# Two chained matrix products on one core: the first product's operands from bfloat16 to float32r

## Chip, cores, metric

One NeuronCore of a Trainium2 chip. The metric is device time in microseconds (us), from profiled and unprofiled executions of the whole kernel; lower is better. Unless said otherwise, the *pitch* of matmuls is the distance between the start times of neighbouring matmul records in the trace, and a *full-clock* pitch is one taken where the records of the granted TensorE clock stand at 1.0.

## The reference

```python
# x (16, 512, 768), w1 (768, 3072), b1 (3072), w2 (3072, 768), all float32
y = np.matmul(x, w1) + b1
y = np.maximum(y, 0)
return np.matmul(y, w2).astype(np.float32)
```

## The kernel before

The 8192 rows of x go through in 16 blocks of 512. Per block: 24 transposes of 128x128 on the TensorE (PE) bring x into the layout that the PE contracts over, the VectorE (DVE) copies them from PSUM to SBUF, 144 matmuls make the first product (24 tiles of hidden units, 6 steps of contraction), the ScalarE (ACT) adds the bias and applies the ReLU, and 192 matmuls make the second product. Everything that the PE reads is bf16; the loads on the gpsimd queue cast.

```python
w1_sb = const_pool.tile([P, KS, H], BF16)
ident = const_pool.tile([P, P], BF16)
xload_pool: bufs=8   xt_pool: bufs=3   yt_pool: bufs=2   osb_pool: bufs=6
tr_psum:    bufs=2   mm1_psum: bufs=2  mm2_psum: bufs=4      # PSUM

def load_xblock(blk):                       # 4 tiles of 128 rows
    xl = xload_pool.tile([P, K], BF16, name="xl")
    nc.gpsimd.dma_start(out=xl, in_=xf[m0 + ms * P: ..., :])

def transpose_xblock(xls):
    xt = xt_pool.tile([P, KS, M_BLK], BF16, name="xt")
    for ms in range(MSUB):                  # 4 groups
        trp = tr_psum.tile([P, KS, P], BF16, name="trp")
        for k in range(KS):                 # 6 transposes each
            nc.tensor.transpose(trp[:, k, :],
                                xls[ms][:, k * P:(k + 1) * P], ident)
        nc.vector.tensor_copy(out=xt[:, :, ms * P:(ms + 1) * P], in_=trp)
    return xt

def mm1(xt):
    for ht in range(HS):                    # 24
        for k in range(KS):                 # 6
            nc.tensor.matmul(ps, lhsT=w1_sb[:, k, ht * P:(ht + 1) * P],
                             rhs=xt[:, k, :], start=(k == 0), stop=(k == KS - 1))
        nc.scalar.activation(out=yt[:, ht, :], in_=ps, func=Relu, bias=...)
# mm2: 4 output tiles of 48 matmuls of 384 columns, two DVE copies, one DMA each
# ... cut ...
for blk in range(NBLK):
    xt = transpose_xblock(xls_next.pop(0))
    if blk + 2 < NBLK:
        xls_next.append(load_xblock(blk + 2))
    yt = mm1(xt)
    mm2(blk, yt)
```

(The pool lines are shortened here.)

## Time and profile before

1066.14 us (median of 2 runs, 1066.07 to 1066.21). The numbers that matter:

| in the steady state, per block of 65.0 us | us |
|---|---|
| boundary: first transpose to first matmul of the first product | 2.72 |
| first product, 144 matmuls at a pitch of 216 ns | 31.08 |
| second product, 192 matmuls at a pitch of 162.5 ns | 31.20 |

Sixteen such blocks are 1040 us; the other 26 us are the start (first x; then matmuls at half clock, 427 ns apart up to 14.7 us; waiting for w2) and the end. The clock's records begin only at 14.7 us, so the row PEclk below does not show that first stretch.

The page of the profile, its busy times, its chain of waits (the work that ended last, followed back) and the costliest groups. A group line has line, engine, operation, output<-inputs, shapes and count, then busy us, mean ns of one, and the idle time of the engine before them with what ended it.

```profile
PE 1033.2 (97%) x5760; PEld 551.0 (52%) x5760; DVE 96.9 (9%) x192; ACT 265.2 (25%) x385; POOL 67.1 (6%) x118
...
PEclk9999999999999999999999999999999999999999
...
PE 91%; DMA 4%; DVE 3%; POOL 1%; issue 0%; DVEq 0%; POOLq 0%
PE mm2p L112 46%; PE mm1p L95 44%; DMA w_sb<-in_w_dram 4%; DVE osb L117 1%; DVE xt L77 1%; POOL w_sb L82 1%; PE trp L75 1%; POOL xl L65 0%; DVEq L162 0%; POOL ident masks.py:199 0%; POOL ident masks.py:197 0%; POOLq masks.py:199 0%; POOLq L151 0%
...
L112 PE MATMUL mm2p<-w_sb,yt 128*128 128x384 bf16 x3072 | 506.2, 327 | 6.8 <-DMA w_sb<-in_w_dram 6.3
L95 PE MATMUL mm1p<-xt,w_sb 128*128 128x512 bf16 x2304 | 502.1, 380 | 3.9 <-DVE xt L77 3.9
...
L117 DVE COPY osb<-mm2p 128x384 f32<-128x384 f32 x128 | 65.3, 551 | 945.0 <-PE mm2p L112 945.0
...
L75 PE MATMUL trp<-ident,xl 128*128 128x128 bf16 x384 | 30.2, 224 | 17.6 <-DVE xt L77 11.2
L75 PEld LDWEIGHTS <-xl 128*128 128x128 bf16 x384 | 24.8, 100 | 23.6 <-issue 13.0
L77 DVE COPY xt<-trp 128x768 bf16<-128x768 bf16 x64 | 32.8, 549 | 20.4 <-PE trp L75 18.6
```

The PE is busy 97% of the span and 90% of the chain that ended last are the two products. The mean of a matmul record (380 ns) is longer than its pitch, since matmuls overlap in the pipeline; that is why pitches are used here. A stretch of the first product in the timeline (start, duration, group, count) shows it: 20 matmuls in 4.48 us, so (4.48 - 0.38) / 19 = 216 ns each. The Trainium skill, "TensorE: Matmul & The Clock Gate", section "Back-to-back issue gap", gives N / 2.4 + 2.5 ns for the gap of an isolated matmul of N moving columns at full clock, 215.8 for 512, and about 131 ns for 512 columns in a stream of weight loads and matmuls: this trace is such a stream, and agrees with the first figure, not with the second.

```profile
299.76 4.48 PE L95 MATMUL mm1p<-xt,w_sb 128*128 128x512 bf16 x20
```

One boundary, from the timeline of before:

```profile
214.83 1.63 PE L112 MATMUL mm2p<-w_sb,yt 128*128 128x384 bf16 x9
...
216.30 0.83 PE L75 MATMUL trp<-ident,xl 128*128 128x128 bf16 x12
216.34 1.02 DVE L117 COPY osb<-mm2p 128x384 f32<-128x384 f32 x2 [6.78 <-PE mm2p L112]
...
217.27 2.15 DVE L77 COPY xt<-trp 128x768 bf16<-128x768 bf16 x4
...
217.87 0.96 PE L75 MATMUL trp<-ident,xl 128*128 128x128 bf16 x12 [0.74 <-DVE xt L77]
...
219.02 2.32 PE L95 MATMUL mm1p<-xt,w_sb 128*128 128x512 bf16 x10 [0.18 <-DVE xt L77]
```

Two groups of transposes go at once, because there are two PSUM buffers; the DVE first copies the last output tiles, then four transposed tiles without a gap. The PE waits 0.74 and 0.18 us. One of the four groups belongs already to the next block, which is why the first product can start before the fourth copy ends.

### The profile page before, as it was taken

How to read it: one execution, taken by the hardware profiler on the slowest of the kernel's cores; microseconds unless marked ns; L12 is line 12 of the kernel's file. 1: busy time of each engine (PE TensorE's matmuls, PEld its weight loads, DVE VectorE, ACT ScalarE, POOL GpSimd, SP SyncE). 2: the span in 40 equal slices, each digit the busy share in tenths (PEclk: the TensorE clock that was granted, in tenths of full speed). 3: DMA queues.
4: the chain of work that ended last, by engine and by line, in shares of the span. 5: the costliest groups of instructions: out<-in, count | busy, mean ns of one | idle time of the engine just before them, and what ended most of it. 6: DMA issues, size and time to landing. Idle time of an engine off the chain costs nothing.

```text
span 1066.0 us, 12515 instructions
## 1 busy us (share of the span) xinstructions
PE 1033.2 (97%) x5760; PEld 551.0 (52%) x5760; DVE 96.9 (9%) x192; ACT 265.2 (25%) x385; POOL 67.1 (6%) x118
## 2 busy tenths in 40 slices
PE   7889999999999999999999999999999999999998
PEld 3344554645546455454555545455464554545554
DVE  1011010110101101020010101101011010100101
ACT  3303205032140412305123050321404214041230
POOL 7510000000000000000000000000000000000000
PEclk9999999999999999999999999999999999999999
DMA  9962030120301202011020201203012020100001
GB/s 158 195 129 60 16 75 1 45 45 15 75 1 45 45 30 60 1 54 37 30 60 15 69 7 43 47 16 74 1 46 45 19 64 1 45 15 31 30 1 60
DMA packets 43844, 48.00 MB, mean 45 GB/s; under 512 B 24336, under 2 KB 35600, under 8 KB 43792
## 3 DMA queue, kind: packets, MB, share of 16 engines
q0 software_dynamic: 31488, 22.03, 14.2%
q1 hardware_dynamic: 12304, 25.18, 6.3%
q8 instruction: 45, 0.74, 0.3%
q14 instruction: 7, 0.06, 0.0%
HBM read 44.05 MB, written 25.17 MB: 65 GB/s over the span
## 4 chain that ended last, share of the span: by engine, by line
PE 91%; DMA 4%; DVE 3%; POOL 1%; issue 0%; DVEq 0%; POOLq 0%
PE mm2p L112 46%; PE mm1p L95 44%; DMA w_sb<-in_w_dram 4%; DVE osb L117 1%; DVE xt L77 1%; POOL w_sb L82 1%; PE trp L75 1%; POOL xl L65 0%; DVEq L162 0%; POOL ident masks.py:199 0%; POOL ident masks.py:197 0%; POOLq masks.py:199 0%; POOLq L151 0%
## 5 line engine op out<-in xcount | busy, mean ns | idle before, releaser
L112 PE MATMUL mm2p<-w_sb,yt 128*128 128x384 bf16 x3072 | 506.2, 327 | 6.8 <-DMA w_sb<-in_w_dram 6.3
L95 PE MATMUL mm1p<-xt,w_sb 128*128 128x512 bf16 x2304 | 502.1, 380 | 3.9 <-DVE xt L77 3.9
L99 ACT ACTIVATE yt<-mm1p,b_sb 128x512 bf16<-128x512 f32 x384 | 263.9, 687 | 759.6 <-PE mm1p L95 759.6
L112 PEld LDWEIGHTS <-yt 128*128 128x128 bf16 x3072 | 301.1, 98 | 211.0 <-issue 12.3
L95 PEld LDWEIGHTS <-w_sb 128*128 128x128 bf16 x2304 | 225.7, 98 | 275.4 <-issue 8.1
L117 DVE COPY osb<-mm2p 128x384 f32<-128x384 f32 x128 | 65.3, 551 | 945.0 <-PE mm2p L112 945.0
L65 POOL DMA_DIRECT2D xl<-in_x_dram x64 | 34.1, 538 | 785.5 <-PE trp L75 780.4
L75 PE MATMUL trp<-ident,xl 128*128 128x128 bf16 x384 | 30.2, 224 | 17.6 <-DVE xt L77 11.2
L75 PEld LDWEIGHTS <-xl 128*128 128x128 bf16 x384 | 24.8, 100 | 23.6 <-issue 13.0
L77 DVE COPY xt<-trp 128x768 bf16<-128x768 bf16 x64 | 32.8, 549 | 20.4 <-PE trp L75 18.6
L82 POOL DMA_DIRECT2D w_sb<-in_w_dram x24 | 19.7, 836 | 5.2 <-DMA w_sb<-in_w_dram 4.6
L87 POOL DMA_DIRECT2D w_sb<-in_w_dram x24 | 12.7, 531 | 10.7 <-DMA w_sb<-in_w_dram 10.7
L99 ACT ACT_TABLE_LOAD x1 | 1.3, 1283 | 6.1 <-DMA b_sb<-in_b_dram 6.1
masks.py:199 POOL TENSOR_SCALAR_AFFINE_SELECT ident<-ident 128x128 bf16<-128x128 bf16 x1 | 0.3, 306 | 0.1
masks.py:197 POOL MEMSET ident<- 128x128 bf16 x1 | 0.2, 205 | 0.3 <-POOLq L151 0.3
L151 POOL MEMSET const-float32-0.0<- 128x1 f32 x1 | 0.1, 99 | 0.2 <-issue 0.2
L151 POOL MEMSET const-bfloat16-1.0<- 128x1 bf16 x1 | 0.1, 103 | 0.0
L151 POOL MEMSET const-uint8-127<- 128x1 uint8 x1 | 0.1, 103 | 0.0
L151 POOL MEMSET const-float32-1.0<- 128x1 f32 x1 | 0.1, 99 | 0.0
## 6 DMA issues: line engine op xcount, KB each, us to landing
out_dram<-osb SPq DMA_DIRECT2D x64, 384.0 KB, 2.3
xl<-in_x_dram POOLq DMA_DIRECT2D x64, 192.0 KB, 5.3
w_sb<-in_w_dram POOLq DMA_DIRECT2D x48, 192.0 KB, 7.8
b_sb<-in_b_dram SPq DMA_DIRECT2D x1, 12.0 KB, 5.3
```

The source lines that it names most:

```text
L65: nc.gpsimd.dma_start(out=xl, in_=xf[m0 + ms * P: m0 + (ms + 1) * P, :])
L75: nc.tensor.transpose(trp[:, k, :], xls[ms][:, k * P:(k + 1) * P], ident)
L77: nc.vector.tensor_copy(out=xt[:, :, ms * P:(ms + 1) * P], in_=trp)
L82: nc.gpsimd.dma_start(out=w1_sb[:, :, ht * P:(ht + 1) * P], in_=w1r[:, :, ht * P:(ht + 1) * P])
L87: nc.gpsimd.dma_start(out=w2_sb[:, h, :], in_=w2[h * P:(h + 1) * P, :])
L95: nc.tensor.matmul(ps, lhsT=w1_sb[:, k, ht * P:(ht + 1) * P], rhs=xt[:, k, :], start=(k == 0), stop=(k == KS - 1))
L99: nc.scalar.activation(out=yt[:, ht, :], in_=ps, func=mybir.ActivationFunctionType.Relu, bias=b1_sb[:, ht:ht + 1])
L112: nc.tensor.matmul(pss[j], lhsT=yt[:, h, ms * P:(ms + 1) * P], rhs=w2_sb[:, h, j * NF:(j + 1) * NF], start=(h == 0), stop=(h == HS - 1))
L117: nc.vector.tensor_copy(out=osb[:, j * NF:(j + 1) * NF], in_=pss[j])
L151: nc = _bacc.Bacc("TRN2", target_bir_lowering=False, num_devices=1)
```

## The change

Its intent: the first product is to read its operands at more than bf16's precision, as float32r. x is then loaded and transposed as float32, and w1 is kept as float32r. The wider tiles need room, so pools shrink: a transposed group of 6 x 128 columns takes 3072 bytes of PSUM per partition instead of 1536, and there is one such buffer instead of two.

```diff
-    w1_sb = const_pool.tile([P, KS, H], BF16)
+    w1_sb = const_pool.tile([P, KS, H], FP32R)
-    ident = const_pool.tile([P, P], BF16)
+    ident = const_pool.tile([P, P], FP32)
-    xload_pool ... bufs=8      xt_pool ... bufs=3      osb_pool ... bufs=6
+    xload_pool ... bufs=4      xt_pool ... bufs=2      osb_pool ... bufs=4
-    tr_psum ... bufs=2
+    tr_psum ... bufs=1
-            xl = xload_pool.tile([P, K], BF16, name="xl")
-            nc.gpsimd.dma_start(
+            xl = xload_pool.tile([P, K], FP32, name="xl")
+            nc.sync.dma_start(
-        xt = xt_pool.tile([P, KS, M_BLK], BF16, name="xt")
+        xt = xt_pool.tile([P, KS, M_BLK], FP32R, name="xt")
-            trp = tr_psum.tile([P, KS, P], BF16, name="trp")
+            trp = tr_psum.tile([P, KS, P], FP32, name="trp")
```

(Pool lines shortened.)

## The prediction

> **What bounds it now.** The TensorE. The page gives PE 97% busy; the chain of waits is 46% second product (L112), 44% first product (L95). In the steady state a block takes 65.0 us (start times in the trace): a boundary of 2.72 us (24 transposes, waiting for DVE copies), 144 matmuls of the first product at a start-to-start pitch of 216 ns = 31.1 us, 192 of the second at 162.5 ns = 31.2 us. 16 x 65.0 = 1040; the other 26 us are the start: first x tile at 5.9 us, cold matmuls, and about 11 us of the first block's second product waiting for w2. Weight loads (PEld, 98 ns each) are hidden.
>
> **What the change does.** It removes nothing from the PE.
>
> 1. First product, 2304 matmuls (all critical). I expect the pitch to stay near 216 ns (single pass). The risk is the weight load: the Trainium skill, "TensorE: Matmul & The Clock Gate", section on weight-path perf modes, says Fast Weight Load is on when the number of weights is 128 and the dtype is not FP32, and no run here shows where float32r falls. An unaccelerated load still hides behind 216 ns if it can be pulled ahead; if not, I estimate 55 to 110 ns more per matmul, 15 blocks x 144 = +119 to +238 us. Hiding 65%, exposure 27%, a half-rate moving stream (about +450 us) 8%.
>
> 2. Transposes are now true float32 (x and identity); now 56 ns pitch warm. Its "FP8 and Floating Point Precision", TensorE Precision Notes, gives true FP32 four passes; if that holds for transposes, about 224 ns each (estimate: 4 x 56), six per tile 1.3 us.
>
> 3. The PSUM copy goes from bf16 768 (546 ns) to f32 768. The f32 384 copy takes 551 ns, so with some 150 ns fixed I estimate 950 ns.
>
> 4. One transpose buffer instead of two: transposes and copies strictly alternate, and the instruction order shows that the group transposed ahead for the next block is gone. The boundary becomes about 4 x (1.3 + 0.95 + 0.05) = 9.2 us instead of 2.7 (7 if transposes take one pass, 13 if their weight loads are exposed too). +6.5 us x 15 = +97 us (range +62 to +160).
>
> 5. Clock: a boundary of 7 to 9 us with a thinly used array may lower the granted clock for a 3.4 us window, as once in before at 62.5 us, while w2 was awaited: 0 to 2 us per block, +10 us in sum.
>
> 6. x loads by the SP queue: off the path. The first block's end is set by w2's arrival (about 62 us, same HBM bytes), so block 0 hides up to about 11 us of slower work; hence 15 blocks, not 16.
>
> **Sum:** 1066 + 97 + 10 + a little for weight loads = about 1185 us; 8 in 10 within 1130 to 1360. Faster by over 2%: 1%; within 2%: 2%; slower: 97%.
>
> **What would show it.** Pitch of L96 matmuls (216 or about 300); count and pitch of transposes (384 or more records); DVE copy near 950 ns; wait of the transposes for DVE near 16 x 4 us, from 11 us in all; first transpose of a block to its first matmul 9 us; PEclk below 9 at block starts.
>
> **What would make it wrong.** Weight loads of float32r not overlapped (1300 to 1420 us); a half-rate moving operand (1600); transposes in a fast single pass (1140).

## The result

1222.38 us (median of 2 runs, 1221.99 to 1222.78) against 1066.14: the ratio is 1.1465, with a 95% interval of 1.1443 to 1.1487. Here and below a ratio is the mean time of one kernel's fast runs over that of the other's of the same rounds, so it is not quite the ratio of the medians quoted.

The page after, the same lines as above, and the weight loads of the first product:

```profile
PE 1139.3 (93%) x5760; PEld 801.3 (66%) x5760; DVE 125.3 (10%) x192; ACT 265.1 (22%) x385; POOL 33.2 (3%) x54
...
PEclk9979999989899898998989999899998989989899
...
PE 88%; DVE 6%; DMA 5%; issue 1%; POOL 0%; DVEq 0%; POOLq 0%
PE mm1p L96 44%; PE mm2p L113 40%; DMA w_sb<-in_w_dram 5%; DVE xt L78 5%; PE trp L76 4%; DVE osb L118 1%; POOL w_sb L83 0%; POOL w_sb L88 0%; DVEq L163 0%; POOL ident masks.py:199 0%; POOL ident masks.py:197 0%; POOLq masks.py:199 0%; POOLq L163 0%; POOLq L152 0%
...
L96 PE MATMUL mm1p<-xt,w_sb 128*128 128x512 f32 x2304 | 568.5, 409 | 16.8 <-DVE xt L78 16.8
L96 PEld LDWEIGHTS mm1p<-xt,w_sb 128*128 128x128 f32 x2304 | 451.0, 197 | 132.5 <-DVE xt L78 22.6
L113 PE MATMUL mm2p<-w_sb,yt 128*128 128x384 bf16 x3072 | 511.2, 328 | 4.3 <-DMA w_sb<-in_w_dram 3.7
...
L118 DVE COPY osb<-mm2p 128x384 f32<-128x384 f32 x128 | 65.4, 552 | 1024.6 <-PE mm2p L113 1024.6
L76 PE MATMUL trp<-ident,xl 128*128 128x128 f32 x384 | 65.1, 314 | 55.5 <-DVE xt L78 51.0
L76 PEld LDWEIGHTS trp<-ident,xl 128*128 128x128 f32 x384 | 49.6, 159 | 68.7 <-DVE xt L78 62.8
L78 DVE CAST xt<-trp 128x768 fp32r<-128x768 f32 x64 | 61.1, 955 | 67.0 <-PE trp L76 67.0
```

Read against before: PE busy time fell from 97% to 93% of a longer span, the transposes now have 55.5 us of idle time before them (17.6 before), and DVE copies went from 549 to 955 ns. The row PEclk (the granted clock, in tenths; it was 9 in every slice before) has a 7 in block 0 and from there on 8s among its 9s (a block takes two and a half slices). The second product kept its count and its mean (328 ns).

The same stretch of the first product in the timeline: 19 matmuls in 4.59 us, (4.59 - 0.39) / 18 = 233 ns each.

```profile
119.63 4.59 PE L96 MATMUL mm1p<-xt,w_sb 128*128 128x512 f32 x19
```

One boundary after. Transposes and copies take strict turns: each group of six waits about a microsecond for the copy of the one before, since there is one buffer.

```profile
165.74 2.76 PE L113 MATMUL mm2p<-w_sb,yt 128*128 128x384 bf16 x16
...
168.34 0.82 PE L76 MATMUL trp<-ident,xl 128*128 128x128 f32 x6
...
169.31 0.95 DVE L78 CAST xt<-trp 128x768 fp32r<-128x768 f32 x1
...
170.32 0.87 PE L76 MATMUL trp<-ident,xl 128*128 128x128 f32 x6 [1.16 <-DVE xt L78]
...
171.23 0.96 DVE L78 CAST xt<-trp 128x768 fp32r<-128x768 f32 x1 [0.97 <-PE trp L76]
...
172.24 0.87 PE L76 MATMUL trp<-ident,xl 128*128 128x128 f32 x6 [1.05 <-DVE xt L78]
...
176.09 5.08 PE L96 MATMUL mm1p<-xt,w_sb 128*128 128x512 f32 x14 [1.05 <-DVE xt L78]
```

From 168.34 to 176.09 is 7.75 us, where before took 2.72. Then the clock. One block of the changed kernel in three stretches (boundary, first product, second product); the columns are the stretch, its length, busy us and count of PE, PEld, DVE, ACT and POOL, and then the granted clock, the DMA share and GB/s:

```profile
317.81:326.23 8.42, 4.11 (x25) 3.00 (x24) 4.76 (x6) 0.00 (x0) 0.00 (x0) 0.84 0.67 189
326.23:361.84 35.61, 35.61 (x144) 28.43 (x145) 0.00 (x0) 15.81 (x23) 0.00 (x0) 0.94 0.04 11
361.84:393.05 31.21, 31.21 (x193) 18.85 (x193) 3.07 (x6) 0.69 (x1) 0.00 (x0) 1.00 0.10 39
```

A mean of 0.84 over 8.42 us and 0.94 over 35.61 us means a clock at one half during about 2.7 and 4.3 us: the records show one stretch of 6.83 us at 0.5, across the start of the first product. Such stretches follow 13 of the 15 boundaries after the first block, 3.41, 6.83 or 10.24 us long. In the records of before, none follows a boundary. (In block 0, while w2 is awaited, the clock is lowered for 17.1 us in the changed kernel and 3.4 us in before.)

Added up from the start times, over the whole profiled span (1065.9 to 1220.9, +155.0 us):

| where | before | after | difference |
|---|---|---|---|
| block 0 with the start, up to the first transpose of block 1 | 86.3 | 96.2 | +9.9 |
| 15 boundaries, the part they would take at full clock (5.83 + 14 x 7.76 after) | 40.8 | 114.5 | +73.7 |
| 15 first products, the part at full clock (15 x 33.71 after) | 466.2 | 505.7 | +39.5 |
| lowered clock in those boundaries (7.3) and first products (24.0) | 0 | 31.3 | +31.3 |
| 15 second products, and the end | 472.7 | 473.3 | +0.6 |

33.71 us for a first product at full clock is what the undisturbed blocks of this run and of e3 and e9 below take. The attribution of these rows to causes is what the experiments test.

### The profile page after: what moved, and what is told of

It is laid out like the page before. It is cut to its first block, busy times and chain, and to the rows that moved or that the text cites. A ratio compares the mean times of both kernels' runs of the same rounds, so it can differ in the third digit from the quotient of the medians.

```text
span 1220.9 us, 12612 instructions
## 1 busy us (share of the span) xinstructions
PE 1139.3 (93%) x5760; PEld 801.3 (66%) x5760; DVE 125.3 (10%) x192; ACT 265.1 (22%) x385; POOL 33.2 (3%) x54
## 4 chain that ended last, share of the span: by engine, by line
PE 88%; DVE 6%; DMA 5%; issue 1%; POOL 0%; DVEq 0%; POOLq 0%
PE mm1p L96 44%; PE mm2p L113 40%; DMA w_sb<-in_w_dram 5%; DVE xt L78 5%; PE trp L76 4%; DVE osb L118 1%; POOL w_sb L83 0%; POOL w_sb L88 0%; DVEq L163 0%; POOL ident masks.py:199 0%; POOL ident masks.py:197 0%; POOLq masks.py:199 0%; POOLq L163 0%; POOLq L152 0%
## 5 line engine op out<-in xcount | busy, mean ns | idle before, releaser
L96 PE MATMUL mm1p<-xt,w_sb 128*128 128x512 f32 x2304 | 568.5, 409 | 16.8 <-DVE xt L78 16.8
L96 PEld LDWEIGHTS mm1p<-xt,w_sb 128*128 128x128 f32 x2304 | 451.0, 197 | 132.5 <-DVE xt L78 22.6
L76 PE MATMUL trp<-ident,xl 128*128 128x128 f32 x384 | 65.1, 314 | 55.5 <-DVE xt L78 51.0
L76 PEld LDWEIGHTS trp<-ident,xl 128*128 128x128 f32 x384 | 49.6, 159 | 68.7 <-DVE xt L78 62.8
L78 DVE CAST xt<-trp 128x768 fp32r<-128x768 f32 x64 | 61.1, 955 | 67.0 <-PE trp L76 67.0
```

The lines of the kernel that those rows point to most:

```text
L76: nc.tensor.transpose(trp[:, k, :], xls[ms][:, k * P:(k + 1) * P], ident)
L96: nc.tensor.matmul(ps, lhsT=w1_sb[:, k, ht * P:(ht + 1) * P], rhs=xt[:, k, :], start=(k == 0), stop=(k == KS - 1))
```

## The experiments

The theory: three separate costs per block. (1) One PSUM buffer makes transposes and copies alternate. (2) float32r operands raise the pitch of the first product from 216 to 233 ns. (3) The thinly used boundary lowers the granted clock. The chief rivals: the clock or the float32 transposes explain the higher pitch; or the clock falls because float32 work itself asks for more.

### e1 and e2: one half of the change each

e1 keeps the changed x path and undoes the operands of the product:

```diff
-    w1_sb = const_pool.tile([P, KS, H], FP32R)
+    w1_sb = const_pool.tile([P, KS, H], BF16)
-        xt = xt_pool.tile([P, KS, M_BLK], FP32R, name="xt")
+        xt = xt_pool.tile([P, KS, M_BLK], BF16, name="xt")
```

> The changed kernel, but w1 and the transposed x are bf16 again; x, identity, transposes and their single buffer stay float32. Theory (three separate costs per block: boundary +5 to +5.7 us, lowered clock +1.8 us in the first product, float32r pitch +17 ns x 144 = +2.5 us): the first product's unthrottled pitch goes back to 216 ns, boundary stays 7.8 to 8.4 us, the clock is still lowered for one or two 3.4 us windows per block; period about 72.5 us, total 1175 to 1190. Rival (the slower first product is an effect of the clock or of the float32 transposes, not of float32r operands): pitch stays at 231 to 237 ns in full-clock windows and the total stays above 1205.

Measured: 1171.53 us (1167.07 to 1172.75), ratio to before 1.0977, interval 1.0951 to 1.1002. A little below the expected range. Full-clock pitch 216 ns, boundary 7.76 us, lowered clock after 13 of 15 boundaries.

e2 is the kernel before with only the operands of the product as float32r:

```diff
-    w1_sb = const_pool.tile([P, KS, H], BF16)
+    w1_sb = const_pool.tile([P, KS, H], FP32R)
-        xt = xt_pool.tile([P, KS, M_BLK], BF16, name="xt")      # xt bufs=3, osb bufs=6
+        xt = xt_pool.tile([P, KS, M_BLK], FP32R, name="xt")     # xt bufs=2, osb bufs=4
```

> The kernel before, but w1 and the transposed x are float32r; x, identity and transposes stay bf16 with two PSUM buffers, x still loads through the gpsimd queue. Theory: first product pitch 231 to 237 ns, +38 us in all; the copy now writes 4-byte elements and costs about 950 ns, which makes the boundary about 4.3 us (+24 us in all); block 0 some 8 us later since w1 is written at twice the bytes; no lowered clock at boundaries; total about 1135. Rival (pitch is due to clock or transposes): pitch 216, total about 1090 to 1100.

Measured: 1133.51 us (1132.43 to 1134.55), ratio 1.0629, interval 1.0613 to 1.0645. Full-clock pitch median 232, mean 233 ns; copies 946 ns though they read bf16; boundary 3.71 us (expected 4.3); lowered clock after 3 of 15 boundaries (expected none). The same stretch of the first product as above, in e1 (216 ns) and then in e2 (233 ns):

```profile
189.71 4.48 PE L96 MATMUL mm1p<-xt,w_sb 128*128 128x512 bf16 x20
...
189.75 4.59 PE L96 MATMUL mm1p<-xt,w_sb 128*128 128x512 f32 x19
```

What follows: the higher pitch belongs to the float32r operands, not to clock or transposes, which both rivals said. The two halves add 105.2 and 67.2 us, 172 together; the whole change adds 156. About 15 us of the overlap is, by estimate, the slower copy (955 ns in e1, 946 in e2), which lengthens the boundaries in both halves: 15 x (3.71 - 2.72) in e2.

They also split block 0. The second product of block 0 stops waiting for w2 at 62.37 us in before, at 61.43 in e1 and at 68.60 in e2 (70.57 in the changed kernel). So w2 comes late because of w1's type, not because of x. The HBM bytes are the same, but each of the 24 loads of w1 now writes 384 KB instead of 192 and lands later. Loads of w1 and w2 in before, then those of w1 in e2 (KB each, median us from issue to landing):

```profile
w_sb<-in_w_dram POOLq DMA_DIRECT2D x48, 192.0 KB, 7.8
...
w_sb<-in_w_dram POOLq DMA_DIRECT2D x24, 384.0 KB, 10.0
```

That accounts for part of the row of block 0 only: block 0 ends at 86.3 us in before, 88.0 in e1, 91.0 in e2 and 96.2 in the changed kernel, so 3.5 of the 9.9 us come with neither half alone. No run splits them further.

### e3 and e4: the boundary

e3 halves the transpose tile (three transposes) so that two buffers take the place of one:

```diff
-            trp = tr_psum.tile([P, KS, P], FP32, name="trp")           # bufs=1
+            trp = tr_psum.tile([P, KS // 2, P], FP32, name="trp")      # bufs=2, twice per group
```

> The changed kernel with the transpose tile halved (three 128-column transposes each[...]) and two buffers[...], so that transposes overlap copies again. Theory (boundary is strict alternation of transposes and copies): boundary 5.5 to 6 us, bound by eight copies of about 550 ns after the two output copies; lowered clock for fewer windows; total 1155 to 1185. Rival (boundary is bound by the float32 transposes themselves or the copies' data): boundary stays above 7.5 us, total above 1205.

Measured: 1153.75 us (1153.16 to 1154.18), ratio 1.0818, interval 1.0802 to 1.0835: just under the expected range. Boundary 5.17 us, and not one lowered stretch after the 15 boundaries. Compared with the changed kernel's median of another call, 69 us come back with the same data types and the same PSUM. A boundary and the first product after it, to be read against those of the changed kernel above:

```profile
304.45:309.62 5.17, 3.85 (x26) 2.44 (x24) 4.61 (x10) 0.00 (x0) 0.00 (x0) 1.00 0.65 175
309.62:343.33 33.71, 33.71 (x144) 26.95 (x145) 0.41 (x1) 15.80 (x23) 0.00 (x0) 1.00 0.09 32
```

e4 takes the changed kernel and issues one group of the next block's transposes ahead of each of the four output tiles of the second product:

```diff
         for ms in range(MSUB):
+            if xt_n is not None:
+                transpose_group(xls_n, xt_n, ms)      # next block's group ms
             osb = osb_pool.tile([P, N], FP32, name="osb")
```

> The changed kernel, the four transpose groups of the next block issued one each before the four output tiles of the second product, so that their copies hide behind matmuls. Theory: no wait at the boundary, no lowered clock after block 0; period 24 x 0.109 + 144 x 0.2335 + 31.2 = 67.4 us; total about 1113 (1105 to 1120). Rival (the lowered clock comes from the float32 or float32r work itself, not from idle gaps): low-clock windows remain in most blocks, total 1135 or more.

Measured: 1112.95 us (1112.08 to 1113.62), ratio 1.0436, interval 1.0420 to 1.0451, as expected. One block of e4: first product, then second product with the transposes in it.

```profile
164.98:198.72 33.74, 33.74 (x147) 27.12 (x145) 1.02 (x2) 15.80 (x23) 0.00 (x0) 1.00 0.03 12
198.72:232.40 33.68, 33.68 (x217) 21.41 (x216) 6.62 (x10) 0.69 (x1) 0.00 (x0) 1.00 0.29 83
```

The PE is busy all the time, the clock is 1.00, and the period is 67.42 us, from 75.2. So neither float32 transposes nor float32r products lower the clock; the boundary did. Against e8 below (the same structure in bf16, period 63.6 us) what is left is the pitch, 144 x 17 ns, and 24 transposes at 109 instead of 56 ns: 3.7 of the 3.8 us between the periods.

### e7: the buffer count alone, in bf16

```diff
-    tr_psum = ... tc.tile_pool(name="trps", bufs=2, ...)       # kernel before
+    tr_psum = ... tc.tile_pool(name="trps", bufs=1, ...)
```

> The kernel before with a single transpose buffer, everything bf16. Theory: alternation alone costs: boundary about 4.9 us from 2.7, total about 1098 (1090 to 1110) if the clock is not lowered; if gaps of this size already lower it, up to 1.7 us per block more (1125). Rival (the buffer count is irrelevant, the float32 data alone make the boundary long): boundary under 3.3 us, total below 1076.

Measured: 1128.01 us (1127.23 to 1128.77), ratio 1.0576, interval 1.0558 to 1.0593. The boundary is 5.0 to 5.3 us, as expected for alternation, and the clock is lowered after all 15 boundaries, so the higher of the two expected numbers holds. One digit of a pool, with not one data type changed, costs 5.8%. One of its boundaries and the product after it:

```profile
361.16:366.47 5.31, 2.29 (x26) 1.76 (x24) 3.16 (x6) 0.00 (x0) 1.94 (x4) 0.86 0.62 141
366.47:400.16 33.69, 33.69 (x145) 14.70 (x145) 0.00 (x0) 15.81 (x23) 0.18 (x1) 0.92 0.09 13
```

### e9: useless work in the boundary

If thin use lowers the clock, more work should keep it up. e9 is the changed kernel with each transpose done twice into the same place:

```diff
+            for rpt in range(2):
                 for k in range(KS):
                     nc.tensor.transpose(trp[:, k, :], xls[ms][:, k * P:(k + 1) * P], ident)
```

> The changed kernel with every transpose done twice into the same PSUM place (same result), which puts 24 x 0.109 = 2.6 us of useless array work into every boundary. Theory (the clock is lowered because the array is thinly used over the boundary, about a third of the time; at one half it is not): the full-clock boundary grows from 7.76 to about 10.4 us, but low-clock windows become rare, which gives back about 2.4 us per block; total within 1% of the changed kernel (1212 to 1234). Rival (the clock is lowered by the length of the boundary or by float32 work): low-clock windows stay as many or become more, total 1255 to 1275.

Measured: 1228.80 us (1227.61 to 1229.48), ratio 1.1518, interval 1.1498 to 1.1537. That is 6 us above the changed kernel's median, with 384 more transposes (15 x 2.5 us of boundary). One block, to be read against the three lines of the changed kernel above:

```profile
320.32:330.58 10.26, 6.06 (x49) 5.11 (x48) 4.85 (x6) 0.00 (x0) 0.00 (x0) 1.00 0.49 155
330.58:364.29 33.71, 33.71 (x145) 26.95 (x145) 0.00 (x0) 15.80 (x23) 0.00 (x0) 1.00 0.04 12
364.29:395.50 31.21, 31.21 (x194) 18.84 (x194) 3.07 (x6) 0.69 (x1) 0.00 (x0) 1.00 0.10 39
```

The clock stays at 1.00, and the three stretches sum to 75.18 us against 75.24: the useless transposes cost what the lowered clock had cost. The boundary is longer than ever and the clock does not fall, so the length alone does not lower it, nor does float32 work; what changed is how much of the time the array works.

### e12: cheaper transposes

x, identity and the PSUM tile of the transposes as float32r (x loads through the gpsimd queue, as the casting loads do):

```diff
-            xl = xload_pool.tile([P, K], FP32, name="xl")
+            xl = xload_pool.tile([P, K], FP32R, name="xl")     # nc.gpsimd.dma_start
-            trp = tr_psum.tile([P, KS, P], FP32, name="trp")
+            trp = tr_psum.tile([P, KS, P], FP32R, name="trp")
+    nc.vector.tensor_copy(out=ident, in_=ident_f)      # ident FP32R
```

> The changed kernel with x, identity and the transposes' PSUM tile as float32r instead of float32 (x then loads through the gpsimd queue). Theory (the transposes' 109 ns is the price of exact float32, twice 128 columns): float32r transposes have a pitch of 56 to 61 ns, the full-clock boundary shrinks from 7.76 to about 6.5 us, total about 1205. Rival (109 ns is the price of loading 128 four-byte weights): pitch stays 105 to 112 ns, boundary 7.8 us, total within 1% of the changed kernel.

Measured: 1221.64 us (1221.38 to 1221.90), ratio 1.1454, interval 1.1431 to 1.1477: no gain over the changed kernel, though the transposes did become cheaper (pitch 87 ns in the median at full clock, 127 at half; 109 and 213 as float32). Theory and rival both missed the pitch (56 to 61, and 105 to 112), and the theory missed the total (1205). Boundaries are 7.4 to 8.0 us, and now all 15 are followed by a lowered stretch, of 6.83 or 10.24 us, and a first product takes 36.2 us on the mean instead of 35.3. What the transposes saved, the clock took: less work in a boundary of nearly the same length.

The runs in one table. e5 and e6, of a later section, are in it too. The array's share is 24 transposes (48 in e9, 12 in e5 and e6) times their full-clock pitch, over the full-clock boundary (in e12, which has none, the shortest boundary); it is worked out from the records.

| run | boundary us | array's share | boundaries followed by a lowered clock |
|---|---|---|---|
| before | 2.72 | 49% | 0 of 15 |
| e3 halved tiles | 5.17 | 51% | 0 of 15 |
| e9 doubled transposes | 10.26 | 51% | 0 of 15 |
| e6 blocks of 256 rows, bf16 | 1.58 | 43% | 0 of 30 |
| e2 operands only | 3.71 | 36% | 3 of 15 |
| e5 blocks of 256 rows, float32r | 3.90 | 34% | 8 of 30 |
| changed kernel, and e1 | 7.76 | 34% | 13 of 15 |
| e12 float32r transposes | 7.4 | 28% | 15 of 15 |
| e7 one buffer in bf16 | 5.0 | 27% | 15 of 15 |

The share over the boundary does not sort these rows alone: at 34 to 36% the clock falls after most boundaries or after few. The records say more. In every run the lowered stretches start on one grid of 3413 ns, to within 3 ns. A block of the changed kernel (75.13 us) is 22.01 such lengths, so its boundaries meet the grid nearly alike, and 15 boundaries are not 15 independent trials. Cut on its grid, a run falls into windows, and each window has its own share of work (estimate: a matmul counts as half of its pitch at half clock, which is 427 ns for 512 columns, 320 for 384, 213 for 256 and for a float32 transpose, 127 for a float32r and 107 for a bf16 transpose). In 13 runs (all but e10), after block 0:

| a window with this share of work | is followed by a window at half clock |
|---|---|
| at full clock, under 34% | 51 of 51 |
| at full clock, 34 to 40% | 17 of 35 |
| at full clock, over 40% | 0 of 3843 |
| at half clock, under 70% | 44 of 44 |
| at half clock, 70 to 80% | 5 of 10 |
| at half clock, over 80% | 0 of 64 |

So length matters in one way: a boundary of 3.7 or 3.9 us (e2, e5) is little longer than a window, and the clock falls only where one window lies almost wholly in it. Before's 2.72 us leave every window at 58% or more. And e9 escaped narrowly: its lowest window has 38%.

### e5, e6, e10, e11: where the 17 ns per matmul come from

e5 and its bf16 control e6 make blocks of 256 rows, so that a matmul has 256 moving columns for the same 128 weight columns:

```diff
-    M_BLK = 512
+    M_BLK = 256
```

> The changed kernel with blocks of 256 rows: the first product has 4608 matmuls of 256 columns instead of 2304 of 512; same arithmetic. Theory W (a float32r matmul cannot start sooner than about 231 ns after the one before because its weight load takes 188 ns and starts only when the matmul before starts): full-clock pitch stays near 231 ns, first product doubles, total about 1720 to 1760. Rival R (moving float32r data stream 8% slower): pitch about 116 ns, total 1190 to 1240. Rival F (a fixed 17 ns per matmul): pitch about 125 ns, total 1230 to 1280.

> Control for the run above: the kernel before with blocks of 256 rows, bf16. All theories: pitch near 110 ns (107 for 256 columns plus 2 to 3), total within 2% of before (1060 to 1085).

Measured: e5 1264.53 us (1263.91 to 1266.65), ratio 1.1862, interval 1.1844 to 1.1879; e6 1112.30 us (1112.16 to 1112.71), ratio 1.0431, interval 1.0416 to 1.0447. The control missed its total: inside a group of six the pitch is 109 ns as expected, but the step from group to group takes 145 ns on the mean (a wait that I put down to the two PSUM buffers, which no run tests), and that is 36 ns x 768, 28 of the 46 us above before. So the totals say nothing between the rivals (e5's fell by accident into the range of F), and I read the pitch inside groups: 120 ns in e5 (median; 121 on the mean without a wait of about 200 ns that falls into every second group) against 109.

At 512 columns float32r costs 233 against 216, 17 more; at 256, 11 more. Theory W is refuted: matmuls start 120 ns apart, far under 231, so a weight load of 188 ns does not bound them. Rival F, the same 17 ns for each matmul, would give 126 or more at 256 columns, and is refuted too. The extra grows with the moving columns.

e10 goes to blocks of 128 rows:

```diff
-    M_BLK = 512
+    M_BLK = 128
```

> The changed kernel with blocks of 128 rows, so that the first product's matmuls have 128 columns. Look only at the pitch inside a group of six at full clock (between groups PSUM and ScalarE will make it wait; the total is of no interest, I expect 1450 to 1800). Theory M (moving float32r costs about 0.448 ns per column plus 4 ns, the line through 118.8 ns at 256 and 233.5 ns at 512): pitch about 61 ns. Rival W (the load of 128 float32r weights has a throughput floor): pitch 105 ns or more, as the float32 transposes' 109 ns.

Measured: 2287.4 us (2 runs), outside the range that I gave for the total. Inside groups the pitch is 112 ns at full clock and 213 at half. The whole first product of this kernel and its weight loads:

```profile
L96 PE MATMUL mm1p<-xt,w_sb 128*128 128x128 f32 x9216 | 1557.6, 352 | 78.4 <-DVE xt L78 73.4
L96 PEld LDWEIGHTS mm1p<-xt,w_sb 128*128 128x128 f32 x9216 | 1546.1, 267 | 94.9 <-DVE xt L78 88.7
```

The line of theory M (61 ns) is refuted, and the number is that of rival W: float32r matmuls of 128 columns do not go below about 112 ns, where bf16 transposes of 128 columns have 56. That the weight load sets this floor is not shown: e12's float32r transposes load 128 weight columns of four bytes too, at a pitch of 87 ns. This also spoils the line that I had drawn through 256 and 512 columns: 120 ns at 256 lies close to that floor, so it is an upper limit of what the moving data need. In 1220 of the 2285 us the clock was lowered, although the matmuls follow each other: it fell after 38 of 63 boundaries, each time for 30.7 us, to beyond the end of the first product. A likely reading, by the windows above, is that 128 columns are 107 ns of work in a pitch of 213, about half, too little for the clock to come back.

e11 is e4 with half the weight columns and all 512 moving columns (wrong result):

```diff
-                nc.tensor.matmul(ps, lhsT=w1_sb[:, k, ht * P:(ht + 1) * P], ...
+                nc.tensor.matmul(ps[:64], lhsT=w1_sb[:, k, ht * P:ht * P + 64], ...
```

> The spread version of the changed kernel (e4) with only 64 of the 128 weight columns in every matmul of the first product; wrong result on purpose (half of the hidden units are zero). 512 moving columns as before. Theory M (the moving stream sets the pitch): full-clock pitch stays at 230 to 238 ns. Rival C (reading the weights takes bandwidth from the moving stream): half the weights, half the extra: pitch about 224 ns or less. The total is of no interest (1100 to 1125).

Measured: full-clock pitch 231 ns on the mean and in the median (in e4: 234 and 232). The weight loads became shorter, as they should (135 from 189 ns), and the pitch hardly followed:

```profile
189.76 4.56 PE L97 MATMUL mm1p<-xt,w_sb 128*64 128x512 f32 x19
```

So reading the weights is the smaller part of the 17 ns: half of them bring 3 ns, all of them, if the rest counts alike, 6 to 7 (estimate). One more observation fits a limit in the moving data: at half clock the pitch of 512 columns is 427 ns in the changed kernel and in e7's bf16 alike, with no extra. What limits the moving float32r data at full clock stays open; mixed operands (one float32r, one bf16), which would have split the two sides directly, are refused when the program is built.

### e8: spreading the transposes in the kernel before

The same edit as e4, on the kernel before, all in bf16:

```diff
         for ms in range(MSUB):
+            if xt_n is not None:
+                transpose_group(xls_n, xt_n, ms)
             osb = osb_pool.tile([P, N], FP32, name="osb")
```

> The kernel before with the transposes of the next block spread over the second product, as in e4. Theory: boundary shrinks from 2.72 to 24 x 0.056 = 1.34 us, total about 1045 (1040 to 1050), faster than before by 2%. Rival (spreading costs as much in pipeline breaks as it saves): 1060 or more.

Measured: 1045.31 us (1045.07 to 1045.75), ratio 0.9803, interval 0.9788 to 0.9817. It beats both kernels. It is faster by 2.0%; since the interval spans the mark of 2%, the verdict by that mark is unclear, but the interval is far from 1. And it is the fair partner of e4: with the same structure float32r costs 1112.95 - 1045.31 = 67.6 us, where the change as made cost 156.

## Why the prediction was right, and where it was off

It said 1185 (1130 to 1360) and slower; 1222 was measured. Point by point:

- **What bounds it, and that the change removes nothing from the PE: right.** The second product kept 31.2 us per block.
- **Step 1, the pitch of the first product ("I expect the pitch to stay near 216 ns"): too small.** It is 233 ns, +39.5 us in all (e2 shows that it is the operands). The named risk, weight loads that are not hidden, did not come, though the loads got slower (records of 188 ns against 98; their operands in the trace are one run of 128 columns, where bf16 has four of 32). A term of 17 ns was in none of the three cases that it weighed; the sum had it as "a little".
- **Step 2, transposes ("about 224 ns each"): wrong.** They take 109 ns. That is twice the bf16 pitch (56), not four times: the estimate should not have carried the four passes of a true FP32 product over to them.
- **Step 3, the copy ("I estimate 950 ns"): right.** 955, and the fixed part is 2 x 551 - 955 = 147 ns.
- **Step 4, strict alternation ("9.2 us instead of 2.7"): the mechanism was right (e3, e4, e7), the size too large:** 7.76 at full clock, because of step 2. +73.7 us against +97.
- **Step 5, the clock ("+10 us in sum"): the mechanism was right (e9), the size too small:** 31.3 us outside block 0. It was taken as 0 to 2 us per block; it came after 13 of 15 boundaries, often two 3.41 us lengths at once.
- **Step 6, block 0 ("hence 15 blocks, not 16"): off.** Block 0 does end with w2, but w2 arrives 8.2 us later, of which e2 shows 6.2 with w1's type alone: its loads write twice the bytes, and "same HBM bytes" was the wrong count. +9.9 us, of which 3.5 are not split.

The sum: 97 + 10 and a little were predicted, 73.7 + 39.5 + 31.3 + 9.9 measured. Errors of both signs met inside a range that leaned up for another reason. The path was foreseen; that 1222 came so near to 1185 is partly luck.

## What to carry to other kernels

When a wider type costs a buffer, cost the lost overlap before the arithmetic: here one PSUM buffer fewer costs 5.8% in bf16 alone. Where the PE must wait at a boundary, ask not only how long but how thinly it works there, since the clock is lowered for the matmuls that follow; work issued early into a dense stretch (e4, e8) removes both. And compare a new data type in the structure that suits it: float32r cost 67.6 us in a spread kernel and 156 as the change was made.

## What the Trainium skill lacked or had wrong

- "TensorE: Matmul & The Clock Gate", "HAM oscillation — how this bites in real kernels": its rule is no PE-idle gaps over about 3.4 us. Here the longest wait inside a boundary of the changed kernel was 1.2 us, and the clock was still halved after 13 of 15 boundaries. The section after it, on PSUM-queue cycling, does tell of short idle times that make the clock swing, but gives no measure. Here the measure was the share of work in one window of 3413 ns: under 34% the clock always fell, over 40% never, and it came back only from 70 to 80% on. The length, 3413 ns and multiples, agrees with the window that Part 1 ("What's actually happening") gives, and the value, one half, with its table.
- The same page, "Part 4: PE-mode transpose", says that for transpose mode the full clock does not engage, as it does not count as PE-busy in the same way. In e9 nothing but more transposes was added to the boundary, and the clock stayed full; the transposes of these kernels (nc.tensor.transpose) count, and they run at full clock (bf16 pitch 56 ns, at half clock 107).
- The same page has no float32r. The runs show a pitch of 233 ns at 512 columns (bf16 216), 120 at 256 (109), and about 112 at 128, with weight-load records of 188 ns (bf16 98), all at full clock; at half clock and 512 columns there is no extra (427 ns).
- "FP8 and Floating Point Precision", "TensorE Precision Notes": it gives true FP32 four passes and does not speak of transposes; the prediction carried them over. The pitch of these float32 transposes is 109 ns, twice the 56 of bf16, and 87 in float32r.
- No page that I read has the cost of writing a cast load at twice the width: loads of w1 landed after 10.0 us instead of 7.8, and the waits for w2 ended 6.2 us later (68.60 from 62.37 us), when only the type of the first product's operands was float32r.
